# A decoder trunk in fp32 on one core: output tiles of one block each with both blocks activated in one slot, and the S3 sums of the down stage formed later from loads of their own

## The chip, the core and the metric

The kernel is one program on one core of a Trainium2 chip. TensorE (PE) multiplies, VectorE (DVE), ScalarE (ACT) and GpSimd (POOL) do the element work, and SyncE (SP), ACT and POOL issue the transfers. The metric is the device time of one execution in microseconds; less is better. Times are medians over runs; the trace comes from one further execution under the profiler.

## What is computed

A hybrid decoder layer in fp32, 1024 tokens by 1024 channels. Cut to what matters here:

```python
z = xn @ w_in                       # 1024 x 8448: a_u, a_v, b_x, b_g, c_q, c_k, c_v, z_gate
out_a = _mixer_a(a_u, a_v, ...)     # gelu(u) * (W_s gelu-and-normalised v)
out_b = _mixer_b(b_x, b_g, ...)     # conv, gated linear recurrence, * gelu(b_g)
out_c = _mixer_c(c_q, c_k, c_v, rel_table)
gates = sigmoid(z_gate)             # three blocks of 1024 columns
merged = gates[0]*(out_a @ p_a) + gates[1]*(out_b @ p_b) + gates[2]*(out_c @ p_c)
x = x + g1 * (merged @ w_out)
xn = modulate(rmsnorm(x))
x = x + g2 * ((gelu(conv(xn @ w_gate)) * (xn @ w_up)) @ w_down)    # w_down: 2816 x 1024
return rmsnorm(x)
```

## The kernel before, in words

**Products.** Every big product runs as a fast product of 2 x 2 blocks with seven block products instead of eight (Strassen's scheme in Winograd's form, steps A11, A12, S1, S2, S3, A22, S4), and each block product is three TensorE products, because every operand is split into a high part in fp32r (`wh`, made by ACT) and the rest (`wl`, made by DVE or POOL): high x high, high x low, low x high. One step of one unit is 12 products of 128x512: a **slot**.

**The projections** (`z`, from about 130 us to 790 us). `Stream` writes the program of PE, ACT, DVE, POOL and SP by slot. A unit is a pair of 128-column blocks, seven slots long (`stream_ws`), or 512 columns in fourteen slots (`stream_ts`, for `a_v` and `c_v`). Its steps are in the order of `FIXED`: A11, A12, S1, S2, S4, S3, A22. Behind each product an evacuation (`evac_fixed`, `unit_evac`) adds the bank into the unit's output tiles `m0` and `m1`, one for each block; A11's evacuation (ACT, L161) is a copy into `m0`, and S2's product goes on in the same bank, so S2 can't start before that copy. `post` returns what follows an evacuation so many slots later: the block's activation (gelu or sigmoid, in place, L680 or L701) and its store to a scratch tensor, issued from ACT. `feed()` puts one piece of other work (the recurrence of branch b: sigmoid, exp and sqrt on ACT) into each slot, ahead of what `post` left. A function that lies in another table set has an ACT_TABLE_LOAD ahead of it. The output tiles come from a pool with the tag `ot`; a tile can be written again when the last store out of it has landed.

**Attention and merge** (about 790 us to 1150 us). `load_head` loads one head's queries and keys from scratch on POOL's queue. Heads with odd numbers use the `ot` tiles.

**Gate and up stage** (to about 1720 us), in eleven rounds of two units, ends with `conv` and `down_tokens`, which write the tokens of the down stage to the scratch tensors `ff`, `ta`, `tb`, `tc`, `td` (stores issued by ACT). The tiles `y`, `up`, `gp` of this stage lie in pools that are closed at its end.

**Down stage** (from about 1707 us on). Seven steps (`STEPS`) of eleven rows each, 77 slots numbered through; step `si` has the slots `11*si` to `11*si + 10`. A row of slot s (`row`) loads its tokens and its weight block on SP at slot s - 5 (`LD`) into a `raw` tile of the ring (four of them), splits them on ACT at s - 3 (`HI`) and on DVE at s - 2 (`LO`), and four tokens groups by three products run at s. The rings `wh` and `wl` have eight tiles each; a row takes two of each. Rows 0 and 1 are loaded ahead of this (`begun`). All is recorded by `at_slot(slot, kind, f)` and written out sorted by slot and kind; each engine takes its instructions in that order, SP's queue too. Step S3 needs the sums A11 - A21 (`held3`, eleven tiles in the pool `sums`, which is opened when the pools of the gate and up stage are closed, in memory that these gave back).

Of the kernel before, what the change touches and what calls it, by code (L numbers as in the profile page):

```python
# [20 lines left out]
P = 128  # L21
S = 1024
# [47 lines left out]
def trunk(ctx: ExitStack, tc: tile.TileContext, I: dict, out: bass.AP, dbg=None):  # L70
# [241 lines left out]
    def stream_ts(gb, tcomb, views, ot, post):  # L312

        u = Unit(views, [4, 256])
        bls, banks, outs = [{}, {}], [{}, {}], [None, None]

        def blocks(p):
            if not bls[p]:
                bls[p].update(zip(("A11", "A12", "A21", "A22"), [r[:, 2 * p:2 * p + 2, :] for r in u.raws]))
            return bls[p]  # L320

        for i, (wn, tn, bk) in enumerate(FIXED):
            its = [u.part(2 * i + p, wn, lambda p=p: blocks(p), [2, 256]) for p in range(2)]
            for t2 in range(2):
                def mm(tn=tn, bk=bk, its=its, t2=t2):
                    fresh = bk not in banks[t2]
                    if fresh:
                        banks[t2][bk] = gb()
                    for i in range(2):
                        t = 2 * t2 + i  # L330
                        sl = slice(t * P, t * P + P)
                        j = 0
                        for k in range(4):
                            th, tl = tcomb[tn][k]
                            wh, wl = its[k // 2]["h"], its[k // 2]["l"]
                            for a, b in ((th, wh), (th, wl), (tl, wh)):
                                pe.matmul(banks[t2][bk][:, 256 * i:256 * i + 256], a[:, sl], b[:, k % 2, :],  # L337
                                          start=(fresh and i == 0 and j == 0), stop=(j == 11), skip_group_check=True)
                                j += 1

                def evac(wn=wn, t2=t2):
                    if outs[t2] is None:
                        outs[t2] = ot()
                    m0, m1 = outs[t2]
                    evac_fixed(wn, banks[t2], (m0[:, 0], m0[:, 1]), (m1[:, 0], m1[:, 1]))
                    return post(t2, m0, m1) if wn == "A22" else []

                u.slots.append((mm, evac))
        return u
# [64 lines left out]
    wk = wk_s.enter_context(tc.tile_pool(name="wk", bufs=1))  # L414

    def ot2():
        t = wk.tile([P, 2, 2, HALF], F32, tag="ot", bufs=2, name="ot")
        return t[:, 0], t[:, 1]

    def xslot(pl, tag, dt=F32R, name="xs"):  # L420
        return (pl[tag] if isinstance(pl, dict) else pl).tile([P, HALF], dt, tag=tag, bufs=8, name=name)
# [254 lines left out]
    def project(col, dst, f, j):  # L676

        def post(i, m):
            flat = m.rearrange("p a b -> p (a b)")
            return [(1, lambda: act.activation(flat, flat, f)), (2, lambda: nc.scalar.dma_start(dst[j + i], flat))]  # L680

        return stream_ws(gb1, tcomb, pair_views(col, j), ot2, post)

    def project_rows(j):

        cc = [512 * j, 512 * j + 256]
        dsts = [(v_scr, COL["cv"], c, None) if c < W else (av_scr, COL["av"], c - W, AF.Gelu_apprx_tanh) for c in cc]
        views = [kview(I["w_in"], col + c, 256, 512 * kh, 512 * kh + 512)
                 for (_, col, c, _) in dsts for kh in range(2)]

        def post(t2, m0, m1):
            def store(m, dst, c):
                for h in range(2):
                    r0 = h * HALF + 2 * t2 * P
                    nc.scalar.dma_start(dst[r0:r0 + 2 * P, c:c + 256].rearrange("(a p) c -> p a c", p=P),
                                        m[:, h].rearrange("p (a c) -> p a c", a=2))

            res = []
            for m, (dst, _, c, f) in zip((m0, m1), dsts):
                if f:  # L700
                    res.append((1, lambda m=m, f=f: act.activation(m, m, f)))  # L701
                res.append((2 if f else 1, lambda m=m, dst=dst, c=c: store(m, dst, c)))
            return res

        return stream_ts(gb1, tcomb, views, ot2, post)

# [346 lines left out]
    def load_head(h):  # L1053
        if h % 2 == 0:
            qp = heads["hd"].tile([P, S], F32R, tag="qp", bufs=1, name="qp")
            kk = heads["hd"].tile([P, 2, S], F32R, tag="qk", bufs=1, name="qk")
        else:
            qp, kk = [wk.tile([P, 2, S], F32R, tag="ot", bufs=2, name="qk") for _ in range(2)]
            qp = qp[:, 0]
        nc.gpsimd.dma_start(qp, qk_scr["q"][h].rearrange("c b s -> (c b) s"))  # L1060
        for i in range(2):
            nc.gpsimd.dma_start(kk[HD * i:HD * i + HD], qk_scr["k"][h].rearrange("c b s -> b c s"))
        kh, kl = kk[:, 0], kk[:, 1]
        bt = heads["hd"].tile([P, 2, 256], F32, tag="bt", bufs=2, name="bt")
        for cfg in range(2):
            row = b_scr[cfg * NH + h:cfg * NH + h + 1, :]
            for q in range(4):
                if cfg == 0:
                    src = bass.AP(tensor=row.tensor, offset=row.offset + 127 - q, ap=[[RW - 4, 32], [1, 256]])
                else:  # L1070
                    src = bass.AP(tensor=row.tensor, offset=row.offset + 127 - 32 * q, ap=[[RW - 1, 32], [1, 256]])
                nc.sync.dma_start(bt[32 * q:32 * q + 32, cfg, :], src)
        return qp, kh, kl, bt
# [556 lines left out]
    def at_slot(s_, kind, f):  # L1630
        todo.append((max(0, s_), kind, f))
# [25 lines left out]
    def row(si, k, need, slot, alone=False):  # L1657
# [4 lines left out]
        def load():  # L1662
# [3 lines left out]
                it["raw"] = down_load(tn, wn, k, lp.tile([P, 2, HALF], F32, tag="lraw", bufs=2, name="lraw"))  # L1666
            else:
                it["raw"] = down_load(tn, wn, k)
            if wn == "A11":
                nc.sync.dma_start(held3[k], block_rows("A21", k))  # L1670
            if wn == "S1":
                nc.sync.dma_start(held[k], block_rows("A22", k))

# [21 lines left out]
            for l, h, src in zip(it["l"], it["h"], it["src"]):  # L1695
                dve.tensor_tensor(l, src, h.bitcast(F32), op=OP.subtract)  # L1696

        def third():
            dve.tensor_tensor(held3[k], it["raw"][:, 1], held3[k], op=OP.subtract)

        if wn == "A11":
            at_slot(need - LO, 2.5 if need <= LO else 2, third)
        at_slot(need - LD, 0, load)
        at_slot(need - HI, 2, high)
        at_slot(need - LO, 2 if need <= LO else 1, low)
# [25 lines left out]
    for si in range(7):  # L1731
# [17 lines left out]
        if si in settled:  # L1749
            c, t0, dh = settled[si]  # L1750
            for tp in range(4):
                t = t0 + tp
                at_slot(slot + 1 + tp, 4, lambda c=c, tp=tp, t=t, dh=dh: settle(cs[c][tp], t, (lo, hi)[dh]))
                at_slot(slot + 2 + tp, 4, lambda t=t, dh=dh: square(t, dh))
                if dh:
                    at_slot(slot + 3 + tp, 4, lambda t=t: finish(t))
                    at_slot(slot + 4 + tp, 4, lambda t=t: store(t))
    alone = [row(6, KH - ALONE + i, end - 6 + 2 * i, end, True) for i in range(ALONE)]

    def last(tp):  # L1760
# [15 lines left out]
    at_slot(6, 0, lambda: nc.sync.dma_start(g2b, bcast_rows(g_rows[5], P, D)))  # L1776
    at_slot(8, 0, lambda: nc.sync.dma_start(fnb, bcast_rows(I["final_norm"], P, D)))
    for t in range(NT):
        at_slot(12 + 2 * t, 0, lambda t=t: nc.sync.dma_start(res[t], x2_scr[t]))
    for _, _, f in sorted(todo, key=lambda x_: x_[:2]):  # L1780
        f()
    sched2.close()
# [23 lines left out]
```

## Time and profile before

| what | value |
|---|---|
| time, median of 3 runs | 1966.98 us (1965.74 to 1968.68) |
| time of the profiled execution | 1959.93 us |
| its span, first to last instruction | 1958.1 us |
| granted TensorE clock over the span | 0.98 of full speed |
| TensorE busy (products) | 95% of the span |
| moved | 313.15 MB, 160 GB/s over the span |

The span is what the trace shows; the time has 1.8 us more around it. A group of rows below shows one view of that trace. "Idle before, releaser" is how long the engine had nothing to run before an instruction, and whose end let it go on.

### The profile page before, as it was taken

To read this page: it belongs to the slowest core of one execution; us is meant where nothing else is said; L and a number is where in the kernel's file an instruction comes from. 1 tells how busy PE (TensorE), PEld (TensorE's weight loads), DVE (VectorE), ACT (ScalarE), POOL (GpSimd) and SP (SyncE) were. 2 spreads that over 40 slices of the span, in tenths; PEclk is the share of its full clock that TensorE was granted. 3 is DMA by queue.
4 is the path that set the end of the run, shared out by engine and by line. 5 is a ranking of instruction groups with operands and counts; after the bars stand their busy time and mean duration, and the time that the engine had idled before them with its cause. 6 is when DMAs were issued, how large, how long until landed. Compare 5 with 4: busy or idle time off the path is not lost.

```text
span 1958.1 us, 26389 instructions
## 1 busy us (share of the span) xinstructions
PE 1856.8 (95%) x9119; PEld 1493.1 (76%) x9119; DVE 1295.8 (66%) x2277; ACT 912.8 (47%) x1689; POOL 633.3 (32%) x1067
## 2 busy tenths in 40 slices
PE   6899998999999999899999999998999999979996
PEld 5677897867777788677777777776888887858885
DVE  5766566556767885555666655579758566667766
ACT  5345456665444444644545433445434343434542
POOL 5320000001311211345656654655545444200001
PEclk9899999999999999899999999999999999989998
DMA  9232423434666768867756256404334333189643
GB/s 322 79 108 100 142 98 129 133 120 156 198 188 198 237 228 250 207 156 177 184 150 164 91 205 214 135 22 140 134 102 130 109 125 101 64 287 324 217 154 121
DMA packets 243078, 313.15 MB, mean 160 GB/s; under 512 B 15991, under 2 KB 166755, under 8 KB 242944
## 3 DMA queue, kind: packets, MB, share of 16 engines
q1 hardware_dynamic: 197520, 186.43, 31.3%
q10 hardware_dynamic: 30384, 75.65, 10.2%
q0 software_dynamic: 15040, 49.38, 9.4%
q8 instruction: 72, 1.18, 0.3%
q14 instruction: 62, 0.51, 0.1%
HBM read 229.47 MB, written 81.93 MB: 159 GB/s over the span
## 4 chain that ended last, share of the span: by engine, by line
PE 78%; DVE 7%; ACT 5%; DMA 4%; issue 3%; POOL 2%; ACTq 0%; SPq 0%; DVEq 0%; POOLq 0%
PE g L298 20%; PE g L191 19%; PE g L1614 10%; PE gp L1158 7%; PE g L337 5%; PE go L1420 4%; PE sl L1225 3%; PE g L215 2%; PE tp L1269 1%; PE o L1298 1%; PE gp L1383 1%; PE o L1301 1%; PE m L790 1%; DVE st L252 1%; ACT wh L254 1%
## 5 line engine op out<-in xcount | busy, mean ns | idle before, releaser
L298 PE MATMUL g<-xs,wh 128*128 128x512 f32 x1344 | 437.7, 407 | 12.0 <-ACT ot L161 12.0
L191 PE MATMUL g<-xs,wh 128*128 128x512 f32 x1176 | 367.9, 394 | 9.5 <-DVE up L168 2.7
L298 PEld LDWEIGHTS g<-xs,wh 128*128 128x128 f32 x1344 | 254.3, 191 | 82.1 <-ACT ot L161 13.7
L298 PE MATMUL g<-xs,wl 128*128 128x512 f32 x672 | 269.1, 400 | 0.0
L191 PEld LDWEIGHTS g<-xs,wh 128*128 128x128 f32 x1176 | 220.5, 188 | 63.0 <-DVE up L168 3.1
L191 PE MATMUL g<-xs,wl 128*128 128x512 f32 x588 | 230.4, 393 | 0.0
L1158 PE MATMUL gp<-oT,wh 128*128 128x512 f32 x512 | 171.6, 415 | 7.3 <-DVE ot L170 3.6
L116 ACT ACTIVATE wh<-raw 128x512 fp32r<-128x512 f32 (+2 forms) x163 | 92.9, 586 | 175.2 <-PE g L191 45.3
L254 ACT ACTIVATE wh<-st 128x512 fp32r<-128x512 f32 x120 | 75.6, 630 | 179.9 <-DVE st L252 179.9
L298 PEld LDWEIGHTS g<-xs,wl 128*128 128x128 f32 x672 | 128.7, 192 | 31.5
L117 POOL TENSOR_TENSOR wl<-st,wh 128x512 fp32r<-128x512 f32 x63 | 101.9, 1618 | 144.7 <-ACT wh L116 139.9
L191 PEld LDWEIGHTS g<-xs,wl 128*128 128x128 f32 x588 | 110.5, 188 | 24.9
L1614 PE MATMUL g<-wh 128*128 128x512 f32 x292 | 114.9, 393 | 14.6 <-ACT wh L1691 14.0
L117 POOL TENSOR_TENSOR wl<-raw,wh 128x512 fp32r<-128x512 f32 (+2 forms) x71 | 92.1, 1298 | 103.0 <-ACT wh L116 100.3
L337 PE MATMUL g<-wh,xs 128*128 128x256 f32 x672 | 124.8, 286 | 0.0
L1614 PE MATMUL g<-wl,wh 128*128 128x512 f32 x292 | 114.9, 393 | 0.6 <-DVE wl L1696 0.6
L1614 PE MATMUL g<-wh,wl 128*128 128x512 f32 x292 | 114.4, 392 | 0.0
L116 ACT ACTIVATE wh<-st 128x512 fp32r<-128x512 f32 x84 | 52.5, 628 | 130.4 <-PE g L191 96.4
L1158 PEld LDWEIGHTS gp<-oT,wh 128*128 128x128 f32 x512 | 89.9, 192 | 30.1 <-issue 7.7
L1691 ACT ACTIVATE wh<-raw 128x512 fp32r<-128x512 f32 x102 | 62.6, 628 | 102.1 <-issue 29.8
L1696 DVE TENSOR_TENSOR wl<-raw,wh 128x512 fp32r<-128x512 f32 x102 | 68.8, 689 | 55.6 <-ACT wh L1691 55.2
L337 PEld LDWEIGHTS g<-wh,xs 128*128 128x128 f32 x672 | 103.8, 188 | 1.6 <-issue 1.4
(331 smaller groups left out, 3922.2 us busy)
## 6 DMA issues: line engine op xcount, KB each, us to landing
raw<-in_w_in_dram SPq DMA_DIRECT2D x66, 512.0 KB, 4.9
raw<-in_f_wdown_dram SPq DMA_DIRECT2D x62, 256.0 KB, 4.3
adaw<-in_w_ada_dram SPq DMA_DIRECT2D x48, 256.0 KB, 5.4
g_scr<-ot ACTq DMA_DIRECT2D x24, 512.0 KB, 3.9
adaw<-in_w_ada_dram POOLq DMA_DIRECT2D x48, 256.0 KB, 4.8
raw<-g_scr SPq DMA_DIRECT2D x24, 512.0 KB, 3.5
qk<-k_scr POOLq DMA_DIRECT2D x24, 512.0 KB, 7.3
raw<-in_f_wgate_dram SPq DMA_DIRECT2D x22, 512.0 KB, 3.8
```

The source lines that it names most:

```text
L116: act.activation(h, src, AF.Copy)
L117: l_eng.tensor_tensor(l, src, h.bitcast(F32), op=OP.subtract)
L191: pe.matmul(banks[bk], a[:, k, :], b, start=(fresh and j == 0), stop=(j == 11), skip_group_check=True)
L254: act.activation(it["h"], bl[name], AF.Copy)
L298: pe.matmul(banks[bk], a[:, k, :], b, start=(fresh and j == 0), stop=(j == 11), skip_group_check=True)
L337: pe.matmul(banks[t2][bk][:, 256 * i:256 * i + 256], a[:, sl], b[:, k % 2, :], start=(fresh and i == 0 and j == 0), stop=(j == 11), skip_g ...
L1158: pe.matmul(pt, a_[:, k % g, :], b_, start=(j == 0), stop=(j == 3 * n - 1))
L1225: pe.matmul(sb[:, of:of + n], lq, kt[:, ks], start=(of == 0 and kt is kh), stop=(kt is kl), skip_group_check=True)
L1420: pe.matmul(pt, a_[:, sl], b_, start=(k == 0 and j == 0), stop=(k == KD - 1 and j == 2))
L1614: pe.matmul(bank, a_[:, sl], b_, start=(start and j == 0), stop=(j == 2), skip_group_check=True)
L1691: act.activation(h, src, AF.Copy)
L1696: dve.tensor_tensor(l, src, h.bitcast(F32), op=OP.subtract)
```

## The change

- `ot2` gives two tiles of one block each (four in the pool) instead of two halves of one tile (two in the pool). The memory is the same.
- `project`: the first block's activation moves from one slot behind S4 to three slots behind it, where the second block's already stands (one slot behind A22), its store one slot on.
- `project_rows`: the first block's activation and store follow S4 instead of A22.
- `load_head`: the keys' high and low parts are tiles of their own, with four transfers of half the size instead of two; odd heads take three `ot` tiles of four instead of two of two.
- Down stage: `held3` no longer comes with the rows of step A11. `third_load` loads A21 and, once more, A11 (into a tile `st` of the ring) in the slots 7 to 21, and the subtraction follows three slots later. The settling of the first token group (`settle`, `square` behind step A12) moves 12 slots back, the eight loads of `res` 8 slots back.

```diff
@@ stream_ts, evac
-                    return post(t2, m0, m1) if wn == "A22" else []
+                    return post(t2, 0, m0) if wn == "S4" else post(t2, 1, m1) if wn == "A22" else []
@@ ot2
-        t = wk.tile([P, 2, 2, HALF], F32, tag="ot", bufs=2, name="ot")
-        return t[:, 0], t[:, 1]
+        return [wk.tile([P, 2, HALF], F32, tag="ot", bufs=4, name="ot") for _ in range(2)]
@@ project
-            return [(1, lambda: act.activation(flat, flat, f)), (2, lambda: nc.scalar.dma_start(dst[j + i], flat))]
+            d = 1 if i else 3
+            return [(d, lambda: act.activation(flat, flat, f)), (d + 1, lambda: nc.scalar.dma_start(dst[j + i], flat))]
@@ project_rows
-        def post(t2, m0, m1):
+        def post(t2, i, m):
...
-            res = []
-            for m, (dst, _, c, f) in zip((m0, m1), dsts):
-                if f:
-                    res.append((1, lambda m=m, f=f: act.activation(m, m, f)))
-                res.append((2 if f else 1, lambda m=m, dst=dst, c=c: store(m, dst, c)))
-            return res
+            dst, _, c, f = dsts[i]
+            if f:
+                return [(1, lambda: act.activation(m, m, f)), (2, lambda: store(m, dst, c))]
+            return [(1, lambda: store(m, dst, c))]
@@ load_head
-            kk = heads["hd"].tile([P, 2, S], F32R, tag="qk", bufs=1, name="qk")
+            kk = [heads["hd"].tile([P, S], F32R, tag="qk", bufs=2, name="qk") for _ in range(2)]
         else:
-            qp, kk = [wk.tile([P, 2, S], F32R, tag="ot", bufs=2, name="qk") for _ in range(2)]
-            qp = qp[:, 0]
+            qp, *kk = [wk.tile([P, S], F32R, tag="ot", bufs=4, name="qk") for _ in range(3)]
         nc.gpsimd.dma_start(qp, qk_scr["q"][h].rearrange("c b s -> (c b) s"))
-        for i in range(2):
-            nc.gpsimd.dma_start(kk[HD * i:HD * i + HD], qk_scr["k"][h].rearrange("c b s -> b c s"))
-        kh, kl = kk[:, 0], kk[:, 1]
+        for c in range(2):
+            for i in range(2):
+                nc.gpsimd.dma_start(kk[c][HD * i:HD * i + HD], qk_scr["k"][h][c])
+        kh, kl = kk
@@ row (down stage)
-            if wn == "A11":
-                nc.sync.dma_start(held3[k], block_rows("A21", k))
...
-        def third():
-            dve.tensor_tensor(held3[k], it["raw"][:, 1], held3[k], op=OP.subtract)
-
-        if wn == "A11":
-            at_slot(need - LO, 2.5 if need <= LO else 2, third)
@@ behind the steps
-                at_slot(slot + 1 + tp, 4, lambda c=c, tp=tp, t=t, dh=dh: settle(cs[c][tp], t, (lo, hi)[dh]))
-                at_slot(slot + 2 + tp, 4, lambda t=t, dh=dh: square(t, dh))
+                at_slot(slot + 1 + tp + 12 * (si == 1), 4, lambda c=c, tp=tp, t=t, dh=dh: settle(cs[c][tp], t, (lo, hi)[dh]))
+                at_slot(slot + 2 + tp + 12 * (si == 1), 4, lambda t=t, dh=dh: square(t, dh))
...
+    a11 = {}
+
+    def third_load(k):
+        a11[k] = ring_tmp([HALF])
+        nc.sync.dma_start(held3[k], block_rows("A21", k))
+        nc.sync.dma_start(a11[k], block_rows("A11", k))
+
+    for k in range(KH):
+        at_slot(10 + 7 * k // 5 - 3, 0, lambda k=k: third_load(k))
+        at_slot(10 + 7 * k // 5, 2, lambda k=k: dve.tensor_tensor(held3[k], a11.pop(k), held3[k], op=OP.subtract))
...
-        at_slot(12 + 2 * t, 0, lambda t=t: nc.sync.dma_start(res[t], x2_scr[t]))
+        at_slot(20 + 2 * t, 0, lambda t=t: nc.sync.dma_start(res[t], x2_scr[t]))
```

In the rows of the order below, line numbers are those of each kernel's own file, which differ by up to two lines for the same statement.

**Place 1: SP's queue where the down stage begins.** Before the change, behind the two rows that are loaded ahead (`raw_15695`, `raw_15698`), the row loads (L1562 tokens, L1564 weights) stand behind loads into `held3`:

```order
418 L1562 DMA raw_15698<-ff1_scr_168 128x512
419 L1564 DMA raw_15698<-in_f_wdown_dram 128x512
420 L1670 DMA held3_15878<-in_f_wdown_dram 128x512
421 L1670 DMA held3_15879<-in_f_wdown_dram 128x512
422 L1562 DMA raw_15911<-ff2_scr_169 128x512
423 L1564 DMA raw_15911<-in_f_wdown_dram 128x512
424 L1670 DMA held3_15880<-in_f_wdown_dram 128x512
425 L1562 DMA raw_15915<-ff3_scr_170 128x512
```

The same place with the change, and the first `held3` load twelve rows further on:

```order
418 L1560 DMA raw_15767<-ff1_scr_168 128x512
419 L1562 DMA raw_15767<-in_f_wdown_dram 128x512
420 L1560 DMA raw_15978<-ff2_scr_169 128x512
421 L1562 DMA raw_15978<-in_f_wdown_dram 128x512
422 L1560 DMA raw_15981<-ff3_scr_170 128x512
...
441 L1560 DMA raw_16173<-ff12_scr_179 128x512
442 L1562 DMA raw_16173<-in_f_wdown_dram 128x512
443 L1753 DMA held3_15947<-in_f_wdown_dram 128x512
444 L1754 DMA st_16176<-in_f_wdown_dram 128x512
```

The loads into `held3` have moved from ahead of row 2 to behind row 12, and eleven loads into `st` are new.

**Place 2: ACT at the end of a gate unit and the start of the unit behind it**, while the recurrence of branch b is being fed in. L271 is S3's evacuation, L161 the next unit's A11 copy, `th` the recurrence's sqrt. Before:

```order
286 L680 ACT_TABLE_LOAD
287 L680 ACTIVATE ot<-ot 128x1024
288 L271 ACTIVATE ot<-g 128x512
289 L254 ACTIVATE wh<-st 128x512
290 L680 DMA g_scr<-ot 128x1024
291 L254 ACTIVATE wh<-st 128x512
292 L805 ACT_TABLE_LOAD
293 L805 ACTIVATE th<-th 128x1024
294 L680 ACT_TABLE_LOAD
295 L680 ACTIVATE ot<-ot 128x1024
296 L161 ACTIVATE ot<-g 128x512
```

With the change:

```order
278 L271 ACTIVATE ot<-g 128x512
279 L254 ACTIVATE wh<-st 128x512 x2
280 L803 ACT_TABLE_LOAD
281 L803 ACTIVATE th<-th 128x1024
282 L680 ACT_TABLE_LOAD
283 L680 ACTIVATE ot<-ot 128x1024 x2
284 L161 ACTIVATE ot<-g 128x512
```

The first block's activation has moved from ahead of L271 to beside the second block's, and the table load that stood ahead of it is gone. Over the whole program L680's 12 table loads become 9.

**Place 3: SP's queue in the first rows of step S1** (`ta` tokens). Before, in the slot of row 5 of that step:

```order
412 L1562 DMA raw_16501<-ta5_scr_194 128x512
413 L1564 DMA raw_16501<-in_f_wdown_dram 128x512
414 L1672 DMA held_15872<-in_f_wdown_dram 128x512
415 L1779 DMA res_15896<-x25_scr_164 128x1024
```

With the change, rows 4 and 5 of that step:

```order
414 L1560 DMA raw_16553<-ta4_scr_193 128x512
415 L1562 DMA raw_16553<-in_f_wdown_dram 128x512
416 L1668 DMA held_15940<-in_f_wdown_dram 128x512
417 L1753 DMA held3_15957<-in_f_wdown_dram 128x512
418 L1754 DMA st_16557<-in_f_wdown_dram 128x512
419 L1560 DMA raw_16586<-ta5_scr_194 128x512
420 L1562 DMA raw_16586<-in_f_wdown_dram 128x512
421 L1668 DMA held_15941<-in_f_wdown_dram 128x512
422 L1780 DMA res_15961<-x21_scr_160 128x1024
```

Two more loads of 256 KB stand between the rows where a `third_load` falls, and the loads of `res` start later (here the second of eight, before the sixth).

## Rows read from the trace of the kernel before

**Rows 1.** The page: span and instructions.
```profile
span 1958.1 us, 26389 instructions
```

**Rows 2.** What TensorE waited for: us in total, times, longest.
```profile
PE g L1614 <- ACT wh L1691: 14.0, 1, 14.0
PE g L298 <- ACT ot L161: 12.0, 3, 4.9
...
PE gp L1158 <- DVE ot L170: 3.6, 1, 3.6
PE gp L1158 <- ACT oT L116: 3.2, 2, 3.0
```

**Rows 3.** Chain that ended last, into the down stage: start, us, what.
```profile
1716.59 2.73 PE g L191 x12
...
1723.98 2.70 DMA td_scr<-y
...
1726.69 0.03 SPq L1670
...
1728.08 4.47 DMA raw<-in_f_wdown_dram
...
1732.58 0.64 ACT wh L1691
...
1733.26 179.54 PE g L1614 x779
```

**Rows 4.** SP's queue from 1690 to 1900 us: us in total, times, longest.
```profile
SPq L1670 <- DMA ff_scr<-up: 49.9, 2, 44.1
```

**Rows 5.** TensorE's timeline: the last product at half pace.
```profile
1738.42 0.47 PE L1614 MATMUL g<-wh,wl 128*128 128x512 f32 x1
```

**Rows 6.** Windows: length, busy of PE, PEld, DVE, ACT, POOL, clock, DMA, GB/s.
```profile
1750.00:1760.00 10.00, 10.00 (x46) 8.29 (x45) 7.99 (x13) 6.67 (x12) 0.00 (x0) 1.00 1.04 393
1770.00:1780.00 10.00, 10.00 (x45) 8.27 (x45) 4.50 (x8) 3.92 (x7) 0.00 (x0) 1.00 0.89 292
1800.00:1850.00 50.00, 50.00 (x222) 41.42 (x221) 39.73 (x64) 27.18 (x52) 1.81 (x3) 1.00 0.74 244
```

**Rows 7.** ACT's timeline at place 2.
```profile
391.09 1.28 ACT L680 ACT_TABLE_LOAD   x1
392.38 1.06 ACT L680 ACTIVATE ot<-ot 128x1024 f32<-128x1024 f32 x1
393.35 0.58 ACT L271 ACTIVATE ot<-g 128x512 f32<-128x512 f32 x1
...
404.10 0.58 ACT L161 ACTIVATE ot<-g 128x512 f32<-128x512 f32 x1
```

**Rows 8.** DVE's timeline behind L271.
```profile
393.96 0.69 DVE L272 TENSOR_TENSOR ot<-g,ot 128x512 f32<-128x512 f32 x1 [4.79 <-ACT ot L271]
```

**Rows 9.** TensorE's timeline: its waits in the projections.
```profile
311.68 1.12 PE L298 MATMUL g<-xs,wh 128*128 128x512 f32 x2 [4.93 <-ACT ot L161]
...
382.38 1.98 PE L790 MATMUL m<-xv,bd 128*128 128x512 f32 x4 [0.98 <-ACT rr L791]
404.74 1.22 PE L298 MATMUL g<-xs,wh 128*128 128x512 f32 x2 [3.51 <-ACT ot L161]
...
454.86 0.96 PE L298 MATMUL g<-xs,wh 128*128 128x512 f32 x2 [3.51 <-ACT ot L161]
```

**Rows 10.** The window around the second of these waits.
```profile
400.00:410.00 10.00, 6.49 (x18) 4.78 (x17) 6.70 (x8) 6.68 (x9) 1.54 (x6) 0.70 0.60 190
```

**Rows 11.** ACT's timeline: copies that wait for a store out of their tile.
```profile
311.03 0.60 ACT L161 ACTIVATE ot<-g 128x512 f32<-128x512 f32 x1 [0.98 <-DMA av_scr<-ot]
...
377.56 0.60 ACT L161 ACTIVATE ot<-g 128x512 f32<-128x512 f32 x1 [2.21 <-DMA av_scr<-ot]
```

**Rows 12.** Groups by line: busy, mean ns, idle before.
```profile
L680 ACT ACT_TABLE_LOAD x12 | 15.4, 1283 | 0.2
...
L1062 POOL DMA_DIRECT2D qk<-k_scr x24 | 14.4, 605 | 9.1 <-PE sl L1225 9.1
```

## The prediction

> **What bounds the kernel now.** The page first: the span is 1958.1 us [rows 1], TensorE has products in 95% of it, and no other engine comes near that. So the question is not which engine is full but where TensorE stands still, and the list of its waits answers it [rows 2]. One wait is 14.0 us long and stands alone: the down stage's first new row, which waits for ACT's split (L1691). Three waits on the copy L161 make 12.0 us, all in the projections. Two more of 3.6 and 3.0 us lie where the projections end and attention begins. Everything else in the list is smaller.
>
> The chain of waits shows what is behind the 14.0 us [rows 3]. The last unit of the up stage ends at 1719.3. Then DVE forms the last token sums, ACT stores them, the last store (`td`) lands at 1726.7, and only then does SP issue its next instruction, L1670, a load into `held3`. Behind it come the tokens and the weights of row 2, which land 4.5 us later, then the split, and TensorE goes on at 1733.26. The stores have nothing to do with row 2: its tokens were written ten rounds earlier. SP's queue tells why it waited: L1670 stood at the head of the queue for 44.1 us [rows 4]. `held3` lies in memory that the gate and up stage's pools gave back, so its first load waits for all that was in them, and the row loads, which need only a free ring tile, wait in line behind it.
>
> TensorE pays for this twice. The first product after the wait starts at 1733.26 and the twelfth at 1738.42 [rows 3, 5]: eleven products in 5.16 us, 0.469 us each. The other 768 products of the 779 in that piece of the chain take 179.54 - 5.16 us, 0.227 us each. So these eleven ran at half clock (1.2 GHz, after 14 us in which TensorE had nothing to do) and cost 5.16 - 11 x 0.227 = 2.7 us.
>
> **The change, part by part.**
>
> *Down stage, what goes.* The order shows that row 2's loads now stand directly behind those of rows 0 and 1. Rows 2 and 3 need the two ring tiles that the up unit's weights held, rows 4 and 5 those of rows 0 and 1, all free before 1707. So all four are there before the up stage ends, and the 14.0 us and the 2.7 us go: 16.7 us.
>
> *Down stage, what comes.* The rings `wh` and `wl` have eight tiles, and the rows 2 and 3 take the last four that the up unit frees; row 3's second split must wait until S4, the unit's last product, has run. ACT's split is 0.64 us [rows 3] and DVE's, of the same shape as the sum in [rows 8], 0.69: together 1.33 us, while TensorE has five products of row 2 left (1.1 us), so 0.2 us shows. In order behind ACT's earlier splits, the copy L167, which frees a bank, comes one split later: 0.6 us. I take 0.8 us, at least 0, at most both whole: 2.0. The last stores (`ta` to `td`) now stand between splits, but their tokens are read twenty rows later and more.
>
> *S3's sums.* Eleven more loads of 256 KB, none saved on the way: the A21 loads were there already. In slots 17 to 27 SP has 33 loads of rows, 6 of `third_load` and 4 of `res` (two units each): 47 x 262144 bytes = 12.3 MB in 11 slots of 12 x 0.227 = 2.73 us, 30.0 us: 411 GB/s. Slots 7 to 16 need 16 + 20 + 2 (`fnb`): 38 units, 365 GB/s. The most that the trace shows for ten microseconds is 393 GB/s, with DMA share at 1.04 [rows 6]. At 393 the slots 17 to 27 take 31.3 us: 1.3 us late. Loads are issued five slots ahead of their products and split three ahead, so a delay up to about two slots (5.5 us) is hidden, and the slots behind need less (22 units in seven slots, 302 GB/s). I take 0. DVE's eleven subtractions move from slots in which it was waiting to slots 10 to 24, 0.69 us in a slot of 2.73 that has two splits (1.4) and at times one sum (0.7) already; the settling that was there is moved away. I take 0.
>
> *Projections.* TensorE's three waits on L161 are waits for one bank: S2 may not start before A11's copy [rows 9]. The copy is late because ACT is. At the second of them ACT's chain can be read backwards [rows 7, 8]: L161 at 404.10, ahead of it the second block's table load and gelu or sigmoid, the recurrence's, the splits that wait for DVE, DVE's L272, which sat idle 4.79 us until L271 had run, and L271, which stood behind a table load (391.09) and the first block's activation (392.38). With the change L271 no longer has these ahead of it: 393.35 - 391.09 = 2.26 us earlier, and the chain to L161 with it. The activation comes back, ahead of L161, without its table load: 1.06 us. Gain there 1.2 to 1.28 us; I take one table load, 1.28 us (15.4 us for 12 of them) [rows 12]. The third wait has the same length and the same chain: 1.28 again. One more table load goes where TensorE isn't waiting: 0.
>
> The Trainium skill ("ScalarE: Activation LUTs", What ACT_TABLE_LOAD costs) puts a switch at 1283 ns and another 1380 ns to drain, 2.66 us. The trace agrees with the first number and shows no second one: the activation starts 1.29 us behind its load [rows 7]. By the page the two would give 5.3 us and the sum would be 2.8 us more; the trace has the duration, so I stay with 1.28.
>
> Where a unit follows `project_rows`, L161 waited for a store out of its tile: 0.98 us at 311 and 2.21 at 377 [rows 11]. With tiles of one block its tile is `m0` alone, whose store now goes four slots earlier. At 311 TensorE waits for just that copy, so 0.98 us. At 377 it doesn't; ACT's chain runs on from there to a wait of 0.98 at 382.38 [rows 9] and to the one at 404. I take 0.98, at least 0, at most 2.21. Sum for the projections: 2 x 1.28 + 2 x 0.98 = 4.5 us.
>
> What can't be read off: whether the clock still falls at these waits when they are shorter. In the window of the second, 18 products started where 45 do in a full one [rows 10, 6]: 27 x 0.227 = 6.1 us lost, 3.5 of them waiting, so the half clock behind it costs 2.6. Three times that is 7.8 us; I take 0.
>
> *The end of the projections.* L271 comes earlier there too, and with it L170, for which TensorE waited 3.6 us. But the next thing that it needs is ACT's splits of `oT`, in the same busy ACT, and there it waited 3.0 us [rows 2]. What comes earlier is waited for again. I take 0, at most 3.6.
>
> *Attention.* 24 more issues on POOL, at 0.605 us [rows 12]: 14.5 us of POOL's time, 1.2 for a head, asked for a head ahead. None of TensorE's long waits is for POOL. I take 0; uncovered at one head, 1.2. The order outside the recorded stretches also shifts by some dozens of products at the start of the projections and of the gate stage: 0, 1 us either way. TensorE's order through attention is the same, row for row.
>
> **Sum.** 16.7 - 0.8 + 4.5 = 20.4 us. The profiled execution took 1959.9 us, so 1939.5 for it. The median of the runs shown is 1967.0, 7 us more than this one; the terms are stalls that every run has, so I take them from the median: **1946.6 us**.
>
> **Rivals.**
>
> *More comes than I count.* The shorter waits keep the clock up (7.8) or L170's 3.6 is real. For it: the waits shrink by a third and more. Against: a third is not the whole. All of it: 1946.6 - 11.4 = 1935; half of it 1941.
>
> *The transfers take some of it back.* If SP's loads in slots 7 to 27 (85 units, 22.3 MB, 57.3 us) run at 292 GB/s, the lowest of the ten-microsecond windows quoted [rows 6], they take 76.3 us: 19.0 late, less 5.5 hidden, 13.5 us of new waits for L1691: 1960.1, still faster by 0.35%. For it: the demand is above anything shown. Against: the 292 is a window in which SP waited for ring tiles, not for transfers. The skill's "DMA: Bandwidth & Descriptors" (Rules for kernel authors) asks for 1 MiB in a transfer to reach full bandwidth, which speaks against four times 256 KB a slot; the 393 GB/s above were reached with 256 KB loads, so here the trace does not bear it out.
>
> *Slower.* The same place, at the 244 GB/s that the trace shows over 50 us [rows 6]: 91.4 us, 34.1 late, 28.6 not hidden, 1946.6 + 28.6 = 1975. It turns to a loss below the rate at which 57.3 + 5.5 + 20.4 = 83.2 us are needed: 268 GB/s.
>
> *The change doesn't do what it says.* Row 2's loads still wait at the head of SP's queue, for a ring tile or a store: then the 15.9 us stay and 4.5 remain, or less with ACT's two activations on end: 1962.5 to 1967, no difference to speak of.
>
> **Chances.** My forecast, with up to 4 us either way, 0.62; more than I count 0.18; the transfers take some back 0.11; doesn't do what it says 0.05; slower 0.04. A measurement of this kernel tells about 0.2% (3.9 us) from no change. Faster is the first three, 0.91; same 0.05; slower 0.04. The range leaves out the far ends: 1938 to 1957, the first three cases without their outer tails.
>
> **What would show it.** Right: TensorE's list has no wait over 2 us for L1691 at the start of the down stage and no half clock behind it; L1753 waits on SP for little; the waits for L161 are two or three, at about 4, 1.5 and 2.2 us; L680 has 9 table loads. Wrong: new waits for L1691 in the rows of step S1 with DMA share at 1 (transfers); SP's row 2 issued after 1720 (head of the queue); L161 waits as long as before (ACT's chain does not move by the table load); a TensorE wait on `qk` (POOL).

## The result, and the profile after

The changed kernel takes 1945.3 us (median of 3 runs, 1944.99 to 1948.24) against 1966.98: ratio 0.9893 (0.9871 to 0.9916). The forecast was 1946.6. Measured once more in five runs it took 1947.1, against 1964.0 for the kernel before: 0.9916 (0.9900 to 0.9932). The kernel before gave 1964.0, 1964.0, 1966.0 and 1964.3 in the later series, so the median of its first three runs stood 1 to 3 us high. The gain is 16 to 22 us by the two measurements; the profiled execution, 1944.99 us, shows where it lies.

Where TensorE waited in the changed kernel (total, times, longest); it answers to [rows 2]:

```profile
PE g L298 <- ACT ot L161: 9.5, 4, 4.1
...
PE gp L1156 <- DVE ot L170: 5.1, 1, 5.1
...
PE gp L1156 <- ACT oT L116: 3.6, 2, 2.5
PE tp L1267 <- DVE pm L1263: 3.5, 2, 2.1
PE sl L1223 <- DVE stat L1228: 3.3, 3, 1.3
...
PE g L1612 <- ACT up L167: 1.0, 1, 1.0
```

The 14.0 us are gone, L161 costs less, L170 more, and two waits inside attention (`tp`, `sl`) are new or longer. The chain that ended last, into the down stage (start, us, what), answers to [rows 3]:

```profile
1713.33 5.29 PE g L1612 x22
1718.62 2.72 PE g L191 x12
1721.34 175.00 PE g L1612 x772
```

The down stage follows the up stage without a gap, and its 772 products take 0.227 us each from the first on: no half clock, where [rows 3, 5] had eleven at 0.469. SP's timeline shows why: behind rows 0 and 1 (1663.30 and 1673.30) the tokens of rows 2 to 5 are issued at 1682.63, 1690.36, 1697.92 and 1704.37, all before the up stage ends, and the first load into `held3` comes at 1732.75:

```profile
1682.63 0.33 SPq L1560 DMA_DIRECT2D raw<-ff_scr  x1
...
1690.36 0.33 SPq L1560 DMA_DIRECT2D raw<-ff_scr  x1
...
1697.92 0.33 SPq L1560 DMA_DIRECT2D raw<-ff_scr  x1
...
1704.37 0.33 SPq L1560 DMA_DIRECT2D raw<-ff_scr  x1
...
1732.75 0.33 SPq L1753 DMA_DIRECT2D held<-in_f_wdown_dram  x1
```

In the slots with the extra loads the transfers run at 357 to 394 GB/s in windows of ten microseconds, at a DMA share of up to 1.05, and TensorE does not stand still (columns as in [rows 6]):

```profile
1770.00:1780.00 10.00, 10.00 (x46) 8.29 (x45) 9.17 (x16) 3.78 (x7) 0.00 (x0) 1.00 1.05 390
...
1790.00:1800.00 10.00, 10.00 (x46) 8.28 (x45) 8.10 (x13) 4.73 (x8) 0.00 (x0) 1.00 1.04 394
```

In the projections the waits of [rows 9] are shorter, and a fourth row, a wait of the merge, serves below as a second mark beside the third wait on L161. First the changed kernel, then the same mark in the kernel before (TensorE's timelines, the wait in brackets):

```profile
309.17 1.22 PE L298 MATMUL g<-xs,wh 128*128 128x512 f32 x2 [4.12 <-ACT ot L161]
...
399.48 0.73 PE L298 MATMUL g<-xs,wh 128*128 128x512 f32 x2 [2.09 <-ACT ot L161]
...
444.61 0.73 PE L298 MATMUL g<-xs,wh 128*128 128x512 f32 x2 [2.08 <-ACT ot L161]
...
1192.03 0.47 PE L1418 MATMUL go<-wh,mh 128*128 128x512 f32 x1 [1.98 <-DVE st L1421]
```

```profile
1193.28 0.47 PE L1420 MATMUL go<-wh,mh 128*128 128x512 f32 x1 [1.97 <-DVE st L1423]
```

At the third wait TensorE is 454.86 - 444.61 = 10.25 us ahead of the kernel before, far more than the waits have shrunk; at the merge only 1.25. Between the two, nine of ten microseconds are given back. L680's table loads are 9 (answers to [rows 12]), POOL's issues for the keys 48:

```profile
L680 ACT ACT_TABLE_LOAD x9 | 11.5, 1283 | 0.3 <-issue 0.2
L1060 POOL DMA_DIRECT2D qk<-k_scr x48 | 25.3, 537 | 23.8 <-PE sl L1223 14.2 <-DVE oT L117 8.4 <-DMA g_scr<-ot 1.2
```

### The profile page after: what moved, and what is told of

It is laid out like the page before. It is cut to its first block, busy times and chain, and to the rows that moved or that the text cites. A ratio compares the mean times of both kernels' runs of the same rounds, so it can differ in the third digit from the quotient of the medians.

```text
span 1943.3 us, 26484 instructions
## 1 busy us (share of the span) xinstructions
PE 1853.5 (95%) x9119; PEld 1490.7 (77%) x9119; DVE 1298.0 (67%) x2277; ACT 910.0 (47%) x1686; POOL 647.7 (33%) x1091
## 5 line engine op out<-in xcount | busy, mean ns | idle before, releaser
L1231 ACT ACTIVATE pm<-pm,stat 128x128 f32<-128x128 f32 (+1 forms) x192 | 88.9, 464 | 34.8 <-DVE stat L1228 28.9
L117 DVE TENSOR_TENSOR wl<-raw,wh 128x512 fp32r<-128x512 f32 (+2 forms) x92 | 73.5, 799 | 47.0 <-ACT wh L116 46.9
```

What stands on the lines that cost most here:

```text
L117: l_eng.tensor_tensor(l, src, h.bitcast(F32), op=OP.subtract)
L1231: act.activation(pm[:, of:of + n], pm[:, of:of + n], AF.Exp, scale=-1.0, bias=stt[:, cfg, 0, idx:idx + 1], accum_out=stt[:, cfg, 1, idx:id ...
```

## The experiments

Theory: the gain in the end is the down stage's; the projections win some ten microseconds, and something between them and the gate stage loses these again. Rivals: "what comes earlier is waited for again" (nothing costs anything by itself), or the keys' transfers cost something by themselves. Ratios are to the kernel before. The two marks in the traces (10 and 11 are left out: their transfers slow attention by another cost):

| kernel | issues for keys | third wait on L161 | wait in the merge | between |
|---|---|---|---|---|
| before | 24 | 454.86 | 1193.28 | 738.4 |
| down stage alone | 24 | 456.30 | 1200.16 | 743.9 |
| four transfers for the keys, alone | 48 | 456.79 | 1207.43 | 750.6 |
| changed | 48 | 444.61 | 1192.03 | 747.4 |
| changed, again | 48 | 444.02 | 1189.56 | 745.5 |
| tiles alone | 48 | 445.32 | 1193.78 | 748.5 |
| changed, activation at once | 48 | 450.82 | 1198.74 | 747.9 |
| changed, head 1 held back | 48 | 443.52 | 1193.38 | 749.9 |
| the same, even heads as before | 36 | 444.31 | 1188.27 | 744.0 |
| changed, one load in front | 48 | 447.27 | 1195.70 | 748.4 |
| changed, more bytes | 48 | 445.38 | 1193.19 | 747.8 |
| changed, first keys twice | 48 | 446.23 | 1195.86 | 749.6 |

**1. The down stage alone.** The kernel before with the diff's hunks from `row` on.

> The kernel before with the down stage's part of the change alone. By the prediction this part is worth 16.7 - 0.8 = 15.9 us: 1951 us against 1967, ratio 0.992, with no wait over 2 us for the split at the start of the down stage and no half clock there. Rival, from the trace of the changed kernel, where the lead over the kernel before is back to nothing when the gate stage begins: this part carries all of the change, some 20 us, ratio 0.990 or lower. A ratio near 1.0 would mean that the wait has another cause than the loads in front of row 2.

1950.2 us, ratio 0.9923 (0.9910 to 0.9936): 15.1 us by the ratio. In its trace the chain runs on as in the changed kernel:

```profile
1728.21 175.00 PE g L1614 x772
```

From the mark in the merge to this chain's end are 1728.21 + 175.00 - 1200.16 = 703.05 us; before, 1733.26 + 179.54 - 1193.28 = 719.52 [rows 3]. The difference, 16.5, is the part's worth, against 15.9 forecast.

**2. The tiles alone.** The other hunks, the down stage as before.

> The kernel before with the output tiles, the activations and the keys' loads of the change, the down stage as before. By the prediction 4.5 us faster: 1962.5 us, ratio 0.9977. Rival, by the changed kernel's trace: TensorE leads by about 10 us at the end of the projections (the waits and 2.7 us of half clock behind three of them), and has lost all of it by the start of the gate stage, to waits for copies and splits where the projections end and for DVE in attention: ratio 0.999 to 1.001. The 14.0 us wait at the start of the down stage stands as before in both.

1962.6 us, 0.9993 (0.9982 to 1.0004): 1.4 us, and the forecast 4.5 lies outside the interval. By the table it leads by 9.5 us at the first mark and is 0.5 behind at the second.

**3. One load back in front of row 2.**

```diff
+            elif (si, k) == (0, 2):
+                nc.sync.dma_start(held3[0], block_rows("A21", 0)); it["raw"] = down_load(tn, wn, k)
...
-        nc.sync.dma_start(held3[k], block_rows("A21", k))
+        nc.sync.dma_start(held3[k], block_rows("A21", k)) if k else None
```

> The changed kernel with one of its 125 loads of the down stage back in front of row 2: the first load into held3, 256 KB. By the prediction's reading (a load at the head of SP's queue that waits for all that was in the memory of the closed pools) this alone brings back the whole wait and the half clock: 14 to 17 us slower than the changed kernel, about 1961, with SP standing some 40 us at that load. Rival (row 2 was late because of the bytes, or because eleven loads stood between the rows): a twenty-second part of it, under 1.5 us.

1961.9 us, 0.9989 (0.9978 to 1.0000): 14 us slower than the changed kernel by the ratios, nearly the whole gain. SP's queue, TensorE's waits and the chain, where 779 products take 179.89 us (179.54 in [rows 3]):

```profile
SPq L1664 <- DMA ff_scr<-up: 50.0, 2, 44.3
```

```profile
PE g L1612 <- ACT wh L1689: 13.3, 1, 13.3
```

```profile
1737.09 179.89 PE g L1612 x779
```

One load of 256 KB at the head of the queue is enough; that it stands there is the cause, not its bytes.

**4. More bytes in slots 7 to 21.** Two copies behind each load into `st`:

```diff
+        for i in range(2):
+            nc.sync.dma_start(g_scr[k][:, HALF * i:HALF * i + HALF], block_rows("A11", k))
```

> The changed kernel with 22 more transfers of 256 KB in the slots 7 to 21 of the down stage (two behind each load into st: a block of weights copied into a scratch tensor that nothing reads any more), 5.8 MB. By the working of the prediction the slots 17 to 27 then ask for 59 units of 262144 bytes in 30 us; at 393 GB/s these take 39.4 us, 9.4 late, of which 5.5 are hidden: 4 us slower than the changed kernel, with waits for the split in step S1. Rival (the loads have room, since TensorE does not wait in this stretch at a DMA share of 1.04): nothing to measure, under 1 us.

1962.0 us, 0.9985 (0.9974 to 0.9997), some 13.5 us slower than the changed kernel by the ratios. The expected 4 us were too few; a likely reason, worked out afterwards, is that only the twelve units of the copies in slots 17 to 27 were counted as late. Over slots 7 to 27 there are 22.3 + 5.8 = 28.1 MB; at 385 GB/s, about what the windows show, 73.0 us in place of 57.3, 15.7 late, less the 5.5 that are hidden: 10.2. The trace has one wait of 9.0 and half clock behind it; it begins with DVE, which waits for late loads while the bank's addition (L1715) stands behind it. Whether the bytes or SP's 22 further issues make the loads late, this run does not tell apart. TensorE's wait, DVE's from 1760 to 1810, and the window:

```profile
PE g L1612 <- DVE c L1715: 9.0, 1, 9.0
```

```profile
DVE held L1683 <- DMA held<-in_f_wdown_dram: 11.9, 7, 3.2
```

```profile
1780.00:1790.00 10.00, 4.90 (x15) 3.95 (x16) 7.33 (x13) 2.83 (x5) 0.00 (x0) 0.66 1.04 389
```

So the rival "the transfers take some of it back" was real and near: the change fits because it needs 22.3 MB in 57.3 + 5.5 us, 355 GB/s, and the changed kernel's windows of ten microseconds from 1740 to 1800 us have 369 to 394.

**5. The changed kernel again.**

> The changed kernel once more, for a ratio from more runs, since the kernel before ranged over 10 us in 29 runs. By the two parts measured alone (0.9923 and 0.9993) the whole is 0.992; by its first measurement 0.989. Expected between the two, 0.989 to 0.992.

1947.1 us, 0.9916 (0.9900 to 0.9932).

**6. The activation back at one slot behind S4** (`d = 1`).

> The changed kernel with the first block's activation back one slot behind S4: tiles of one block as in the change, but L680's table loads are 12 again instead of 9. By the prediction two of TensorE's waits for L161 grow by 1.28 us each and the rest stays: 2.6 us slower at the end of the projections, or 5 to 8 if the clock falls behind them again, as it does in the kernel before. Rival: the shorter waits come from the tiles alone, and nothing changes. Over the whole at most 0.3%, since attention may take it back: read at the end of the projections.

1954.7 us, 0.9949 (0.9936 to 0.9963), some 6.5 us slower than the changed kernel by the ratios. The waits are those of before to the hundredth:

```profile
402.94 0.74 PE L298 MATMUL g<-xs,wh 128*128 128x512 f32 x2 [3.51 <-ACT ot L161]
...
450.82 0.74 PE L298 MATMUL g<-xs,wh 128*128 128x512 f32 x2 [3.51 <-ACT ot L161]
```

Two waits grow by 1.42; the first stays at 4.11 us and the one at 382 stays gone, so these two gains are the tiles' own. From the first wait on L161 to the third this run takes 140.7 us against 135.4, so 5.3 us more, at the lower end of the expected 5 to 8, and nearly half of that is not the waits themselves but small waits and slower products behind them. The 6.5 us are not taken back later: this speaks against "what comes earlier is waited for again".

**7. Four transfers for the keys, alone.** The kernel before with

```diff
-        for i in range(2):
-            nc.gpsimd.dma_start(kk[HD * i:HD * i + HD], qk_scr["k"][h].rearrange("c b s -> b c s"))
+        for c, i in ((0, 0), (0, 1), (1, 0), (1, 1)):
+            nc.gpsimd.dma_start(kk[HD * i:HD * i + HD, c], qk_scr["k"][h][c])
```

> The kernel before with four transfers of half the size for the keys of each head instead of two, into the same tiles: 24 more issues on POOL and nothing else. By the prediction nothing (POOL's 14.5 us are hidden), at most 1.2 us. Rival: POOL's longer queue and the order that the scheduler then gives DVE and ACT in attention cost there what the changed kernel loses between 830 and 1130 us of its trace, 4 us: ratio 1.002.

1977.4 us, 1.0068 (1.0054 to 1.0082): 13 us slower, more than either theory had. Nothing comes earlier here, so this edit costs by itself; that the changed kernel's loss in attention is this cost is argued, since no run has the changed kernel with 24 issues and nothing else. By the table the stretch between the marks is 745.5 to 750.6 us (mean 748.4) in the nine traces with 48 issues, 738.4 and 743.9 in the two with 24: 7.3 us on the mean, though these two differ by 5.5 themselves. In this run's trace TensorE waits 6.7 us for `pm`, for which it has no wait in the kernel before and 3.5 in the changed one:

```profile
PE tp L1269 <- DVE pm L1265: 6.7, 4, 2.5
```

POOL's wait for DVE's reciprocal (L1252 here, L1250 in the changed kernel), from 790 to 1160 us, in this kernel, the changed one and the one before:

```profile
POOL fc L1254 <- DVE nm L1252: 9.4, 11, 2.3
```

```profile
POOL fc L1252 <- DVE nm L1250: 9.7, 11, 2.7
```

```profile
POOL fc L1254 <- DVE nm L1252: 4.2, 10, 1.0
```

One instance, in the changed kernel's timelines of DVE, POOL and TensorE: the sum that the reciprocal needs was formed at 808.68 and took 0.21, but DVE stood at an evacuation that waited for TensorE; the reciprocal ran at 811.32, the factors at 811.59, and TensorE waited for `pm`.

```profile
810.71 0.69 DVE L1166 TENSOR_TENSOR m<-gp,raw 128x512 f32<-128x512 f32 x1 [3.24 <-PE gp L1156]
811.32 0.19 DVE L1250 RECIPROCAL nm<-nm 128x8 f32<-128x8 f32 x1
```

```profile
808.68 0.21 POOL L1249 TENSOR_TENSOR nm<-dd 128x8 f32<-128x8 f32 x1
811.59 0.20 POOL L1252 TENSOR_TENSOR fc<-ex,nm 128x8 f32<-128x8 f32 x1 [2.71 <-DVE nm L1250]
```

```profile
813.91 0.70 PE L1267 MATMUL tp<-ident,pm 128*128 128x128 f32 x3 [1.39 <-DVE pm L1263]
```

In DVE's timeline an evacuation of a merge product (L1166, L1169) stands between the head's step ahead of the sum (`nm<-stat,sw`) and the reciprocal for 6 of the 12 heads in the changed kernel and 6 here, where only the issues differ from the kernel before, which has 1. (The expectations of 10 and 12 count 7 for the changed kernel.) POOL's own time is on this path too: in the same instance its four issues, 2.06 us from 803.38 on, stand ahead of the last copies that the sum needs.

**8. Head 1's loads held back.** One column of head 1's first key tile is written from the last of branch a's columns (`oTs` lists them), so its loads come after that.

```diff
-            qp, *kk = [...]
+            qp, *kk = [...]; h == 1 and pool.tensor_copy(kk[0][:, :1], oTs[-1][:, :1].bitcast(F32))
```

> The changed kernel with the loads of head 1 (1.5 MB into the output tiles) held back until the last of branch a's columns is split: one column of the tile of the keys is first written from that column. Theory of the transfers: with tiles of one block the first two tiles of head 1 come free 22 us earlier against the work than before, its loads then run beside those of branch a's columns, ACT waits 6.5 us for one of these, and the evacuations behind it in ACT's order are late. Then ACT's wait of 6.5 us goes, TensorE's waits between the projections' end and 830 us (5.1 us for L170 and 2.5 to 3.6 for the splits) shrink to what they were before or less, and the kernel is 2 to 5 us faster than the changed one, if attention does not take it back. Rival: what comes earlier is waited for again (ACT's splits and table loads are what takes the time there): the same waits, no difference.

1943.1 us, 0.9896 (0.9882 to 0.9911), not told apart from the changed kernel. ACT's wait of 6.5 us for branch a's columns is gone, though its waits for the merge's weights there grow from 0.6 to 4.1 us, and TensorE still waits 4.4 for L170. Here L271 starts at 777.13, 0.1 us behind the unit's last product, and what is left is DVE's order from there to L170 at 780.61: splits, the first head's L1228, and L272. The theory of the transfers is right on the one wait of ACT and wrong on TensorE. ACT's and TensorE's timelines:

```profile
770.90 0.63 ACT L116 ACTIVATE oT<-oT 128x512 fp32r<-128x512 f32 x1 [0.51 <-DMA oT<-oa_scr]
...
777.13 0.58 ACT L271 ACTIVATE ot<-g 128x512 f32<-128x512 f32 x1
```

```profile
781.43 1.19 PE L1156 MATMUL gp<-oT,wh 128*128 128x512 f32 x2 [4.44 <-DVE ot L170]
```

**9. Head 1's first keys twice** (copied into a scratch tensor as well).

> The changed kernel with two more transfers of 256 KB at that place: the first keys of head 1 are copied a second time, into a scratch tensor that nothing reads any more. Nothing else in any engine's order changes. Theory of the transfers: 524288 bytes at the 310 GB/s or so that move there are 1.7 us; ACT's wait for branch a's columns grows from 6.5 to about 8 us and TensorE's wait for L170 from 5.1 to 6 or 7. Rival: nothing changes there. In the time of the whole at most 2 us, within what runs differ.

1946.3 us, 0.9912 (0.9899 to 0.9926); L170 5.1 as before. It tells nothing: the copies wait for no tile and were issued at 758 and 761 us, ahead of the place that was meant.

**10 and 11. Two transfers for the keys in another form**, in the changed kernel and in that of experiment 8.

```diff
-            for i in range(2):
-                nc.gpsimd.dma_start(kk[c][HD * i:HD * i + HD], qk_scr["k"][h][c])
+            k_ = qk_scr["k"][h][c]
+            nc.gpsimd.dma_start(kk[c], bass.AP(tensor=k_.tensor, offset=k_.offset, ap=[[0, 2], *k_.ap]))
```

> The changed kernel with two transfers for each head's keys instead of four (each reads its 64 rows twice, once for either half of the partitions): POOL has 1072 instructions again, as before the change, and the same bytes arrive. In DVE's order only 2 of the 12 reciprocals of the attention factors (L1250) still stand behind an evacuation that waits for TensorE, as against 7 in the changed kernel and 1 before. Theory of the order: POOL's 24 further issues made the scheduler put those evacuations ahead, the factors come late, and TensorE waits for pm and stat; without them POOL's wait of 9.7 us for L1250 falls to about the 4.2 us of before, TensorE's waits for pm go, and the kernel is 3 to 6 us faster than the changed one: 1941 to 1944. Rival (attention only takes back what came earlier): the same time as the changed kernel, 1947.

> The changed kernel with both edits: two transfers for each head's keys, and the loads of head 1 held back until branch a's columns are split. If the two losses are separate, the gains add: 1947 less 4 less 3 to 6, 1937 to 1940, ratio 0.987. If they are one (attention takes back whatever is won ahead of it), it is no faster than the better of the two, about 1943.

1995.1 us, 1.0148 (1.0135 to 1.0162), and 1992.5, 1.0136 (1.0122 to 1.0150). The edit brought a cost of its own: from 780 to 1150 us a transfer takes 16.5 us to land (first row), against 4.6 for one of half the size in the changed kernel (second) and 7.3 for one of the same size in the kernel before (third):

```profile
qk<-k_scr POOLq DMA_DIRECT2D x21, 512.0 KB, 16.5
```

```profile
qk<-k_scr POOLq DMA_DIRECT2D x42, 256.0 KB, 4.6
```

```profile
qk<-k_scr POOLq DMA_DIRECT2D x22, 512.0 KB, 7.3
```

The Trainium skill ("DMA: Bandwidth & Descriptors", Rules for kernel authors) says that a leading zero-stride dimension of c copies confines a transfer to at most c of the 16 engines; c is 2 here. The slow landing agrees; which engines worked isn't in these rows.

With 24 issues POOL's wait for the reciprocal does fall, to 2.9 us in both, and TensorE's waits for `pm` are gone, as expected; what that is worth can't be read from kernels that are some 45 us slower.

**12. Experiment 8 with even heads as before**: one tile, two transfers, 36 issues in all.

```diff
...
+            if h % 2 == 0:
+                nc.gpsimd.dma_start(kk[HD * i:HD * i + HD], qk_scr["k"][h].rearrange("c b s -> b c s"))
+            else:
+                for c in range(2):
+                    nc.gpsimd.dma_start(kk[c][HD * i:HD * i + HD], qk_scr["k"][h][c])
```

> The changed kernel with the loads of head 1 held back until branch a's columns are split, and with the keys of even heads as before the change: one tile for both parts, two transfers of 512 KB in the form that the kernel before used. POOL has 12 issues fewer than the changed kernel, the bytes are the same. In DVE's order 3 of the 12 reciprocals (L1250) stand behind an evacuation that waits for TensorE, as against 7 in the changed kernel and in the run that this one is built on, and 1 before. Theory of the issues: 24 further issues on POOL and the order that the scheduler makes of them cost the kernel before 13 us when they are added alone; then taking 12 of them away gives back between a third and two thirds of it, 4 to 8 us against the run it is built on (1943): 1935 to 1939, ratio 0.985 to 0.9875, with POOL's wait for L1250 well under 9.7 us. Rival (the losses of attention have to do with when TensorE comes, not with POOL): no difference from that run, 0.9896.

1941.3 us, 0.9884 (0.9865 to 0.9902): the fastest, but 2 us below experiment 8, short of the 4 to 8 expected and within the intervals. Between the marks it takes 744.0 against 749.9, and POOL's wait is down:

```profile
POOL fc L1255 <- DVE nm L1253: 7.0, 10, 2.4
```

In DVE's timeline the evacuation stands ahead of the reciprocal for 3 heads. Of the 5.1 us by which this run is ahead of experiment 8 at the merge, 3.3 are left at the end of the spans (1939.8 against 1943.1 us): where the gate stage starts, one wait for ACT's `gp` is 3.1 us, 1.0 in the other, with slower products behind it. So half of the issues taken away is no proof of their cost.

## Why the time was right, and which steps were not

**Where TensorE stands still: right where it matters.** "Everything else in the list is smaller" is not so: TensorE's waits before 300 us have 7.2, 6.5, 5.4 and 3.7 us in the kernel before. The change does not aim at these, and in the changed kernel they are 7.3, 5.9, 4.8 and 3.3.

**Down stage, what goes (16.7): right**, place, cause and size: 14.0 of wait and the eleven slow products are gone, and experiment 3 brings the wait back with one load. The rows 2 to 5 are issued before 1707, as forecast.

**What comes (0.8): a little less.** L167 costs 1.0 against 0.7, and row 3's second split shows in no wait of its own.

**S3's sums (0): right, with little to spare.** The Trainium skill ("DMA: Bandwidth & Descriptors", Rules for kernel authors), which the prediction weighed, asks for 1 MiB in a transfer; here loads of 256 KB moved 394 GB/s in one window. Experiment 4 shows the price once the cover is used up.

**Projections, the waits (4.5): right.** 4.93 became 4.12 (forecast 0.98 less), 3.51 became 2.09 twice (1.28 each), and the 0.98 at 382 is gone: 4.6 in all; a new wait of 1.2 us lies ahead of them, at 122.68.

**"Whether the clock still falls ... I take 0": mis-sized.** At the third wait the ten traces with the new order (10 and 11 among them) stand at 443.5 to 447.3 (mean 445.2), the three with the old at 454.9 to 456.8 (mean 456.0): 10.8 us. From the first wait to the third the ten take 135.4 to 136.1 us and the three 142.9 to 143.2, so 7.5 us lie there, of which the waits are 3.8 and one of 0.6 at 428 that is gone as well; about 3 us are left, most of it the products behind the second wait, which ran at half clock before. The other 3.3 lie ahead of the first wait; the shorter first wait gives 0.8 of them, and the rest isn't explained. Before, the window with the second wait had a granted clock of 0.83 (first row). Now that wait ends at 399.48, and the window that holds it and the one behind it have 1.00 (second and third row):

```profile
400.00:420.00 20.00, 16.49 (x60) 12.80 (x59) 9.72 (x12) 12.51 (x16) 3.09 (x8) 0.83 0.44 147
```

```profile
380.00:400.00 20.00, 17.91 (x76) 13.98 (x75) 10.40 (x14) 15.48 (x20) 0.65 (x2) 1.00 0.23 77
400.00:420.00 20.00, 20.00 (x85) 15.83 (x85) 16.08 (x21) 10.46 (x16) 3.00 (x7) 1.00 0.46 158
```

Around the third wait (440 to 460 us) the clock was 0.91 before and is 0.91 in the changed kernel too, so it is not the whole 7.8 of the prediction that comes back.

**"24 more issues on POOL ... I take 0; uncovered at one head, 1.2": the step that failed.** It priced the issues as POOL's time, looked only at TensorE's long waits and TensorE's order, and not at what the scheduler does to DVE. Alone they cost 13 us in time, and 7 to 12 between the marks of that trace; the changed kernel's two traces are 5 us longer there than the mean of the two with 24 issues (746.5 against 741.1), so it seems to pay something of that size. How much is POOL's own time, and how much the changed order on DVE, is not settled: taking half of the issues away again (experiment 12) gained 2 us, within the intervals.

**The end of the projections (0): no gain**, as said; the wait for L170 is 3.9 to 6.9 us in the nine traces of the table with the new tiles, 3.2 to 3.9 in the three without.

**The sum.** The tiles were to give 4.5 and give 1.4, because some 6 more than forecast was won up to the third wait and 9 were lost behind it. The down stage was right by itself. The close hit is in part luck: 20.4 us were forecast, and 16.5 came by the ratio of the second measurement (0.9916). With a start of 1964 in place of 1967 the forecast would have been 1943.6, 2 to 3.5 us too fast; the high start covered the terms that were wrong.

## What to carry to other kernels

A load that waits for memory of closed pools belongs behind everything that the next stage needs first; in a queue in order its place costs (experiment 3), not its size. Where a scheduler writes the order, read the order of every engine on the path after an edit: with 24 more issues on POOL alone, an instruction that waits stood ahead of one that TensorE needs for 6 heads in place of 1. Test each part of a change alone even when the total comes out as forecast, since two wrong terms can cancel, as here.

## What was not expected of the hardware

The same instructions differ by more than the terms discussed: between the marks the kernel before took 738.4 us in one execution, and 743.9 in the trace of experiment 1, whose program is the same there. A clock that falls is not decided by the wait alone: the second wait was 3.51 us in the kernel before, with 0.83 granted from 400 to 420 us, and 3.51 in experiment 6, where that window had 1.00.
